# The second half of a channel MLP as seven block products for eight, and the two halves as separate stages

## The chip, the cores and the metric

The kernel runs on one core of a Trainium2 chip. The core has a matrix engine (PE, with its weight loads shown apart as PEld), a vector engine (DVE), an activation engine (ACT), a general engine (POOL) and a queue that issues transfers (SP). The metric is the device time of one execution in microseconds, the median of several. A matrix product writes to PSUM, eight banks of 2 KB for each of 128 partitions; everything else lies in SBUF or in DRAM.

## The reference, cut to what matters

One layer of a diffusion backbone is computed for 128 context tokens and 1024 sample tokens, 1152 together, at a model width of 1024. A mixer (a bidirectional scan and a gated chunk product) comes first. The change concerns what follows, the channel MLP with a squared ReLU, and the norm at the end:

```python
h = rmsnorm(x, norm2_g) * (1 + sc2) + sh2
x = x + g2 * (jnp.square(jax.nn.relu(h @ w_ff1)) @ w_ff2)   # w_ff1 (1024, 4096), w_ff2 (4096, 1024)
...
y_prompt = rmsnorm(xp, final_norm_g)                        # over the 1024 features
```

All inputs and outputs are float32. Each operand of a large product is split into a high part (rounded for the engine) and a low part (the rest), and a product is the sum of three: high by high, high by low, low by high.

## The kernel before, in words

Features lie on the 128 partitions and tokens along the rows, so an activation of 1024 features by 1152 tokens is 8 blocks of 128 rows by 1152 columns. Tokens are worked in three slices of 384 (`SL`, `NS = 3`), the hidden width of 4096 in 32 blocks of 128.

Weights come from DRAM by `wtile` (L171): a transfer of 512 KB on SP into a raw buffer, then `split` (L167), which makes the high part on ACT (a cast) and the low part on POOL (a subtraction), or on DVE where the call says so. `product` (L183) runs 24 matmuls for one output block of 128 by one slice: 8 blocks of the inner width, three matmuls each.

Ahead of the MLP, `norm2(s)` (L933) makes the MLP's input for slice `s`: one matmul with ones sums the squares over the features (`np`), ACT takes the root, DVE the reciprocal, and `modulate` (L206) then makes for each of 8 blocks a scaled value on DVE (`hn`), its high part on ACT (`h22h` for the last slice) and its low part on DVE (`h22l`).

The MLP goes over the hidden width in 16 steps of two blocks (`FB = 2`). `ff1` (L951) makes one hidden block for one slice: a `product`, ReLU on ACT, the square's high part on ACT, the square on POOL, the low part on DVE. `ff2` (L962) multiplies two hidden blocks by their rows of `w_ff2` for all 8 output blocks and 3 slices, 6 matmuls of 384 columns in one PSUM tile each, and `add_scaled` adds the tile to the residual `x1`, which stays in SBUF, by one or two DVE instructions (two where the context and the sample tokens meet in one slice). The two are interleaved: step b of `ff1` is followed by the products of step b-1 in `ff2`, so no hidden block is ever stored.

The last `ff2` call takes the last four hidden blocks and goes over the columns in three pieces (`LAST`: 448, 384 and 320 columns). While it runs, `last` and `final` make the norm of the pieces that are done: sums of squares on ACT, POOL and DVE, root, reciprocal, the scaling on DVE and POOL, and the stores.

From the end of the mixer on, a scheduler sets the order on each engine when the program is built: it takes instructions by the order of the code, lets ready ones pass, and places waits where a buffer is still in use. Each engine then works its own list strictly in that order.

## Time and profile before

| | us |
|---|---|
| median of 3 (1806.94 to 1809.33) | 1807.11 |
| the profiled execution | 1807.15 |
| its span, first to last instruction | 1805.4 |
| first matmul of `ff1` | 982.3 |
| last matmul of `ff2` starts | 1791.3 |

The page gives the busy time of each engine over the span. Matmuls are pipelined: a row's duration (334 ns for 384 columns) overlaps the next row, so what a matmul costs in a stream is the distance between starts. A table by stage gives for each stretch its length, then the busy time of PE, PEld, DVE, ACT and POOL with the count of instructions, then the granted PE clock (1.00 is 2.4 GHz, 0.50 is 1.2 GHz), the busy share of the transfer engines and what they moved; asked for one line, it counts that line's instructions alone. A timeline row has start, duration, engine, line, operation, tiles and sizes, and in brackets the idle time before it with what ended it. A row by shape has the count, the busy time and, after the comma, the mean duration in ns. A row of one tile has the shortest, the median and the longest duration in ns, and the first and last start.

### The profile page before, as it was taken

The numbers are of one execution on the slowest core, as the hardware profiler recorded it, in microseconds if no ns is written. First come the engines' busy times: TensorE is split into PE (matmuls) and PEld (weight loads), VectorE is DVE, ScalarE is ACT, GpSimd is POOL, SyncE is SP. The second block draws the span as 40 slices with busy tenths as digits, with TensorE's granted clock in tenths as the row PEclk, the third lists the DMA queues.
The fourth block names the chain that finished last, engine by engine and source line by source line (L and its number), as shares of the span: only waits on it lengthen the run. The fifth ranks groups of instructions, "written<-read, shape, count | busy, mean of one in ns | idle before, by whom it ended". The sixth has DMA issues, their size and how long they took to land.

```text
span 1805.4 us, 26426 instructions
## 1 busy us (share of the span) xinstructions
PE 1711.6 (95%) x10349; PEld 1644.1 (91%) x10349; DVE 1068.3 (59%) x1551; ACT 669.7 (37%) x1261; POOL 704.3 (39%) x493
## 2 busy tenths in 40 slices
PE   6999998898898988999999999999999999999996
PEld 3888997797888887999999999999999999999996
DVE  5956669969779789575588334344333333444427
ACT  4543446556555555453344411211222221111132
POOL 2300227637537457346555422222233332222234
PEclk9999999999999998999999999999999999999998
DMA  9676333342242364874333111111111111111103
GB/s 348 213 254 212 101 118 101 109 144 96 93 140 85 121 216 148 281 268 133 106 108 103 47 36 47 48 36 37 46 47 47 47 36 36 47 47 36 36 12 106
DMA packets 84925, 193.82 MB, mean 107 GB/s; under 512 B 7584, under 2 KB 47552, under 8 KB 84800
## 3 DMA queue, kind: packets, MB, share of 16 engines
q1 hardware_dynamic: 84800, 192.12, 32.5%
q8 instruction: 82, 1.34, 0.3%
q14 instruction: 43, 0.35, 0.1%
HBM read 157.27 MB, written 34.82 MB: 106 GB/s over the span
## 4 chain that ended last, share of the span: by engine, by line
PE 60%; DVE 14%; issue 5%; ACT 4%; POOL 1%; DMA 1%; DVEq 0%; SPq 0%; ACTq 0%; POOLq 0%
PE fps L190 22%; PE gps L969 21%; PE ops L190 7%; PE ips L190 7%; DVE ap L719 3%; DVE cv L613 2%; ACT ap L722 2%; DVE xwl L169 1%; DVE xw L696 1%; DVE M L724 1%; DVE x L987 1%; PE yp L784 1%; DVE red L929 1%; DVE h20l L216 1%; DVE x L867 0%
## 5 line engine op out<-in xcount | busy, mean ns | idle before, releaser
L867 DVE SCALAR_TENSOR_TENSOR x<-gps,modT,x 128x128 f32<-128x128 f32 (+2 forms) x480 | 232.8, 514 | 122.5 <-PE gps L969 122.5
L960 DVE TENSOR_TENSOR fl<-r,fh 128x384 fp32r<-128x384 f32 x96 | 54.1, 565 | 363.4 <-POOL r L959 363.4
L969 PE MATMUL gps<-fh,w2h 128*128 128x384 f32 (+2 forms) x768 | 257.6, 335 | 1.5 <-DVE x L867 1.5
L969 PE MATMUL gps<-fh,w2l 128*128 128x384 f32 (+2 forms) x768 | 256.9, 334 | 0.0
L969 PE MATMUL gps<-fl,w2h 128*128 128x384 f32 (+2 forms) x768 | 256.8, 334 | 0.0
L169 POOL TENSOR_TENSOR w2l<-w2r,w2h 128x1024 fp32r<-128x1024 f32 x31 | 74.5, 2403 | 324.4 <-ACT w2h L168 324.4
L168 ACT CAST w2h<-w2r 128x1024 fp32r<-128x1024 f32 x32 | 33.6, 1051 | 340.1 <-PE gps L969 314.2
L969 PEld LDWEIGHTS gps<-fh,w2h 128*128 128x128 f32 x768 | 144.2, 188 | 3.0 <-DVE x L867 2.1
L969 PEld LDWEIGHTS gps<-fl,w2h 128*128 128x128 f32 x768 | 144.2, 188 | 0.8 <-issue 0.2
L969 PEld LDWEIGHTS gps<-fh,w2l 128*128 128x128 f32 x768 | 144.1, 188 | 0.6 <-DVE w2l L169 0.2
L959 POOL TENSOR_TENSOR r<-r 128x384 f32<-128x384 f32 x96 | 79.6, 830 | 148.5 <-ACT fh L958 148.5
L169 POOL TENSOR_TENSOR wil<-wir,wih 128x1024 fp32r<-128x1024 f32 x25 | 63.7, 2549 | 161.2 <-ACT wih L168 157.3
L613 DVE SCALAR_TENSOR_TENSOR cv<-xp,cw,cv 128x1156 f32<-128x1156 f32 x64 | 109.7, 1714 | 25.3 <-ACT cv L610 24.1
L722 ACT ACTIVATE ap<-ap,lcol 128x128 f32<-128x128 f32 x288 | 89.4, 391 | 63.8 <-DVE ap L719 63.7
L957 ACT ACTIVATE r<-fps 128x384 f32<-128x384 f32 x96 | 46.8, 489 | 171.5 <-PE fps L190 170.4
L169 POOL TENSOR_TENSOR wol<-wor,woh 128x1024 fp32r<-128x1024 f32 x32 | 80.6, 2525 | 67.6 <-ACT woh L168 67.6
L169 POOL TENSOR_TENSOR w1l<-w1r,w1h 128x1024 fp32r<-128x1024 f32 x32 | 76.8, 2400 | 66.8 <-ACT w1h L168 66.8
L718 POOL TENSOR_TENSOR ea<-ea,cv 128x1024 f32<-128x1024 f32 x32 | 95.2, 2975 | 8.8 <-ACT ea L717 8.8
L190 PE MATMUL ips<-h0h,wil 128*128 128x384 f32 x256 | 90.2, 352 | 0.0
L190 PE MATMUL ips<-h0h,wih 128*128 128x384 f32 x256 | 89.9, 351 | 0.0
L190 PE MATMUL ips<-h0l,wih 128*128 128x384 f32 x256 | 89.9, 351 | 0.0
L190 PE MATMUL ips<-h1h,wil 128*128 128x384 f32 x256 | 88.2, 345 | 0.0
(292 smaller groups left out, 4915.1 us busy)
## 6 DMA issues: line engine op xcount, KB each, us to landing
wa<-in_w_ada_dram SPq DMA_DIRECT2D x48, 512.0 KB, 5.2
wor<-in_w_out_dram SPq DMA_DIRECT2D x40, 512.0 KB, 3.6
ap<-arow_d SPq DMA_DIRECT2D x36, 512.0 KB, 4.9
wir<-in_w_in_dram SPq DMA_DIRECT2D x32, 512.0 KB, 4.0
w1r<-in_w_ff_dram SPq DMA_DIRECT2D x32, 512.0 KB, 3.5
w2r<-in_w_ff_dram SPq DMA_DIRECT2D x32, 512.0 KB, 3.5
mix_d<-vg SPq DMA_DIRECT2D x9, 512.0 KB, 5.2
mxt<-mix_d SPq DMA_DIRECT2D x8, 576.0 KB, 4.5
```

The costliest lines, as they stand in the source:

```text
L168: nc.scalar.copy(hi, src)
L169: lo_eng.tensor_tensor(out=lo, in0=src, in1=hi.bitcast(F32), op=ALU.subtract)
L190: nc.tensor.matmul(ps, a[:, k, :], b[:, k, :], start=n == 0, stop=n == 3 * KD - 1)
L613: nc.vector.scalar_tensor_tensor(out=acc, in0=xp[:, k:k + 1156], scalar=cw[:, 16 * k + m:16 * k + m + 1], in1=acc, op0=ALU.mult, op1=ALU.add)
L718: nc.gpsimd.tensor_tensor(out=ea, in0=ea, in1=G.CT[:, cc(c)].unsqueeze(1).to_broadcast([P, 8, P]), op=ALU.mult)
L719: nc.vector.tensor_tensor(out=ap.rearrange("p (d e) i -> p d e i", d=2), in0=ap.rearrange("p (d e) i -> p d e i", d=2), in1=mask.unsqueeze ...
L722: nc.scalar.activation(ap[:, e, :], ap[:, e, :], AF.Exp, bias=lcol[:, c, 8 * g + e:8 * g + e + 1])
L867: nc.vector.scalar_tensor_tensor(out=x1[m][:, a:b], in0=ps[:, a - cols.start:b - cols.start], scalar=modT[:, g0 + m, v:v + 1], in1=x1[m][: ...
L957: nc.scalar.activation(r, ps, AF.Relu)
L959: nc.gpsimd.tensor_tensor(out=r, in0=r, in1=r, op=ALU.mult)
L960: nc.vector.tensor_tensor(out=fl[:, cs], in0=r, in1=fh[:, cs].bitcast(F32), op=ALU.subtract)
L969: nc.tensor.matmul(ps, a[:, m, :], x[:, cols], start=n == 0, stop=n == n1)
```

## The change

The first half of the MLP becomes a stage of its own. For each pair of hidden blocks it runs 2 by 3 products as before, writes, for each half `q` of the tokens, the ReLU of four sub-blocks (two hidden blocks by two token blocks of `TB = 288`) into a tile of seven places, squares them on ACT, forms three sums and differences on POOL, makes the high part on ACT and the low part on DVE, and stores both, 128 rows by 7 by 288 columns each (1.03 MB), in DRAM (`hid_d`). `norm2` also stores the residual in DRAM (`x1_d`).

Then the first stage's pools are closed and the second half begins. For each of 8 groups of four hidden blocks (`kb`), 4 pairs of output blocks (`m`) and 2 halves of the tokens (`q`) it runs seven block products by a form of Strassen's scheme (Winograd's), each 2 inner blocks by three matmuls of 288 columns. `hidden` loads a group's eight tiles from DRAM into a pool of 11 (`hid`); `w2_blocks` loads four blocks of `w_ff2`, forms the seven weight blocks on POOL, and splits them on ACT and DVE. The products go to two PSUM tiles of four banks each, and `evict` adds them to sums in SBUF (`acc`): four banks after the first four products, three after the other three. In the last group `assemble` makes the output blocks from the seven sums, scales them, adds the residual loaded from DRAM and sums the squares; `final` norms and stores them.

```diff
-    wp = ctx.enter_context(tc.tile_pool(name="wp", bufs=2))
-    hp = ctx.enter_context(tc.tile_pool(name="hp", bufs=6))
+    held = ExitStack()
+    wp = held.enter_context(tc.tile_pool(name="wp", bufs=2, reuse_waits="tile"))
+    hp = held.enter_context(tc.tile_pool(name="hp", bufs=6, reuse_waits="tile"))
...
+        nc.sync.dma_start(x1_d[:, :, scols(s)], x1t[:, :, scols(s)])
...
+    def ff1(f, e, R, after=None):
+        w = wtile(i["w_ff1"][f], "w1")
+        for s in range(NS):
+            ps = mps("fps")
+            product(ps, w, h2[s])
+            for t in range(2 * NQ):
+                a, b = max(t * TB, s * SL), min((t + 1) * TB, (s + 1) * SL)
+                if a < b:
+                    nc.scalar.activation(R[t // 2][:, SLOT[e][t % 2], a - t * TB:b - t * TB], ps[:, a - s * SL:b - s * SL], AF.Relu)
+            if after and s == 1:
+                after()
+    def combine(R, n, q):
+        b11, b21, b22, t1, t2, t3, t4 = (R[:, j, :] for j in range(7))
+        nc.scalar.activation(R[:, 0:4, :], R[:, 0:4, :], AF.Square)
+        for o, x, y, op in ((t3, b22, t1, ALU.subtract), (t1, t1, b11, ALU.subtract), (t2, t3, b11, ALU.add), (t4, b21, t2, ALU.subtract)):
+            nc.gpsimd.tensor_tensor(out=o, in0=x, in1=y, op=op)
+        rh = tl("rh", "rh", (7, TB), F32R)
+        lo = R.bitcast(F32R)
+        split(rh, lo, R, nc.vector)
+        nc.sync.dma_start(hid_d[n][q, 0], rh.bitcast(F32))
+        nc.sync.dma_start(hid_d[n][q, 1], R)
...
+    phase(acc=8, wr=4, wf=2, hid=11)
...
+    def w2_blocks(kb, m):
+        F = tl("wf", "wf", (2, 8, P))
+        for e in range(2):
+            for f, o in ((0, 6), (1, 0)):
+                nc.sync.dma_start(F[:, e, o:o + 2, :], i["w_ff2"][4 * kb + 2 * e + f][:, 2 * m:2 * m + 2, :])
+        a12, a22, s1, s2, s3, s4, a11, a21 = (F[:, :, j, :] for j in range(8))
+        for o, x, y, op in ((s3, a11, a21, ALU.subtract), (s1, a21, a22, ALU.add), (s2, s1, a11, ALU.subtract), (s4, a12, s2, ALU.subtract)):
+            nc.gpsimd.tensor_tensor(out=o, in0=x, in1=y, op=op)
+        wh, wl = (tl("wr", "w2" + x, (2, 7, P), F32R) for x in "hl")
+        split(wh, wl, F[:, :, 0:7, :], nc.vector)
+        return wh, wl
+    def hidden(kb, q):
+        out = []
+        for n in range(2):
+            out.append(tuple(tl("hid", "hid" + x, (7, TB), F32R) for x in "hl"))
+            for z in range(2):
+                nc.sync.dma_start(out[n][z].bitcast(F32), hid_d[2 * kb + n][q, z])
+        return out
+    def products(ps, js, w, h, first):
+        for j in js:
+            b, a, x = BANK[j], W_OF[j], H_OF[j]
             n = 0
-            for (wh, wl), (_, ah, al) in zip(ws, acts):
-                for a, x in ((wh, ah), (wh, al), (wl, ah)):
-                    nc.tensor.matmul(ps, a[:, m, :], x[:, cols], start=n == 0, stop=n == n1)
+            for e in range(2):
+                for wz, hz in ((0, 0), (0, 1), (1, 0)):
+                    nc.tensor.matmul(ps[:, b, :TB], w[wz][:, e, a, :], h[e][hz][:, x, :], start=first and n == 0, stop=n == 5,
+                                     skip_group_check=True)
                     n += 1
-            add_scaled(ps, m, cols, 40)
+    def evict(o, ps, fresh):
+        if fresh:
+            nc.scalar.copy(o, ps)
+        else:
+            nc.vector.tensor_tensor(out=o, in0=o, in1=ps, op=ALU.add)
+    def units(us, kb, done=None):
+        pss = [pf.tile([P, 4, 512], F32, tag="u", name="ups") for _ in us]
+        for (m, q, w, h), ps in zip(us, pss):
+            products(ps, (1, 7, 5, 6), w, h, True)
+            evict(acc[m][q][:, 0:4, :], ps[:, 0:4, :TB], kb == 0)
+        for (m, q, w, h), ps in zip(us, pss):
+            products(ps, (2, 4, 3), w, h, False)
+            evict(acc[m][q][:, 4:7, :], ps[:, 0:3, :TB], kb == 0)
             if done:
-                done(m, cols)
+                done(m, q)
...
+    def assemble(m, q):
+        A = acc[m][q]
+        x = tl("hid", "x", (4, TB))
+        for e in range(2):
+            nc.sync.dma_start(x[:, 2 * e:2 * e + 2, :].rearrange("p a t -> p (a t)"), x1_d[:, 2 * m + e, 2 * q * TB:2 * (q + 1) * TB])
+        nc.vector.tensor_tensor(out=A[:, 0], in0=A[:, 0], in1=A[:, 3], op=ALU.add)
+        nc.vector.tensor_tensor(out=A[:, 1], in0=A[:, 1], in1=A[:, 2], op=ALU.add)
+        nc.vector.tensor_tensor(out=A[:, 5:7], in0=A[:, 5:7], in1=A[:, 0:1].to_broadcast([P, 2, TB]), op=ALU.add)
+        nc.vector.tensor_tensor(out=A[:, 1], in0=A[:, 1], in1=A[:, 0], op=ALU.add)
+        for e, js in ((0, (4, 6)), (1, (5, 1))):
+            for t, j in enumerate(js):
+                for a, b, v in cut((2 * q + t) * TB, (2 * q + t + 1) * TB):
+                    r = slice(a - (2 * q + t) * TB, b - (2 * q + t) * TB)
+                    nc.vector.scalar_tensor_tensor(out=A[:, j, r], in0=A[:, j, r], scalar=modT[:, 40 + 2 * m + e, v:v + 1],
+                                                   in1=x[:, 2 * e + t, r], op0=ALU.mult, op1=ALU.add)
+                if sums[q] is None:
+                    sums[q] = [None, None]
+                sq = tl("hid", "sq", (TB,))
+                nc.scalar.activation(sq, A[:, j], AF.Square)
+                if sums[q][t] is None:
+                    sums[q][t] = sq
                 else:
+                    nc.gpsimd.tensor_tensor(out=sums[q][t], in0=sums[q][t], in1=sq, op=ALU.add)
+    def final(q):
+        for t in range(2):
+            ps = pf.tile([P, 4, 512], F32, tag="u", name="nps")[:, 0, :TB]
+            nc.tensor.matmul(ps, ones, sums[q][t], start=True, stop=True)
+            rs = tl("hid", "rs", (TB,))
+            nc.scalar.activation(rs, ps, AF.Sqrt, bias=eps_t, scale=1.0 / D)
+            nc.vector.reciprocal(rs, rs)
+            for e in range(2):
+                for m in range(4):
+                    o = acc[m][q][:, ((4, 6), (5, 1))[e][t]]
+                    nc.vector.scalar_tensor_tensor(out=o, in0=o, scalar=vcol("final_norm_g", 2 * m + e), in1=rs, op0=ALU.mult, op1=ALU.mult)
+                    nc.sync.dma_start(y_out[2 * m + e, :, (2 * q + t) * TB:(2 * q + t + 1) * TB], o)
...
+    for kb in range(nb - 1):
+        hs = [hidden(kb, q) for q in range(NQ)]
+        for m in range(4):
+            w = w2_blocks(kb, m)
+            units([(m, q, w, hs[q]) for q in range(NQ)], kb)
+    hs = [hidden(nb - 1, q) for q in range(NQ)]
+    for q in range(NQ):
+        for m in (0, 2):
+            units([(k, q, w2_blocks(nb - 1, k), hs[q]) for k in (m, m + 1)], nb - 1, assemble)
+        final(q)
```

Three places show what the scheduler makes of it. The first is PE where the MLP begins; `fps` is an `ff1` product, `h20`, `h21` and `h22` the input of the three slices. Before:

```order
L190 MATMUL fps<-h20h,w1l 128x384
L200 MATMUL np<-red,ones 128x384
L190 MATMUL fps<-h21h,w1h 128x384
L190 MATMUL fps<-h21l,w1h 128x384
L190 MATMUL fps<-h21h,w1l 128x384
```

Now:

```order
L195 MATMUL fps<-h21h,w1l 128x384
L205 MATMUL np<-red,ones 128x384
L195 MATMUL fps<-h22h,w1h 128x384
L195 MATMUL fps<-h20h,w1h 128x384
L195 MATMUL fps<-h20l,w1h 128x384
```

Behind `np` stood 72 matmuls that need only the first two slices; now the next matmul needs the third slice's high part, which `np` leads to.

The second is SP where one group of hidden blocks follows another in the second stage; `hid_d2` and `hid_d3` are the second group's pairs, the first `hidh` and `hidl` of a pair are the token half q = 0, the others q = 1. Before, SP issued in the MLP nothing but the weights of both halves (`w1r`, `w2r`), a step's like the next:

```order
L179 DMA w2r_10949<-in_w_ff2_dram 128x1024
L179 DMA w2r_11351<-in_w_ff2_dram 128x1024
L179 DMA w1r_11563<-in_w_ff1_dram 128x1024
L179 DMA w1r_11571<-in_w_ff1_dram 128x1024
L179 DMA w2r_11357<-in_w_ff2_dram 128x1024
L179 DMA w2r_11759<-in_w_ff2_dram 128x1024
```

Now:

```order
L1013 DMA hidh_12940<-hid_d2_107 128x2016
L1013 DMA hidl_12941<-hid_d2_107 128x2016
L999 DMA wf_12837<-in_w_ff2_dram 128x256 x4
L1013 DMA hidh_12944<-hid_d3_108 128x2016
L999 DMA wf_12956<-in_w_ff2_dram 128x256 x4
L999 DMA wf_13059<-in_w_ff2_dram 128x256 x4
L999 DMA wf_13162<-in_w_ff2_dram 128x256 x4
L1013 DMA hidl_12945<-hid_d3_108 128x2016
L1013 DMA hidh_12948<-hid_d2_107 128x2016
L1013 DMA hidl_12949<-hid_d2_107 128x2016
L1013 DMA hidh_12952<-hid_d3_108 128x2016
L1013 DMA hidl_12953<-hid_d3_108 128x2016
```

Three tiles of the group are loaded ahead; the last five take buffers of the group at work, whose tiles are read until its last pair of output blocks.

The third is DVE at the end; `acc` are the sums of one pair of output blocks, `x` the residual. Before, one instruction followed each product tile, and the last ones were:

```order
L867 SCALAR_TENSOR_TENSOR x1_7337<-gps_15873,modT_115,x1_7337 128x320
L929 TENSOR_TENSOR red_15768<-red_15768,sq_15870 128x320
L929 TENSOR_TENSOR red_15768<-red_15768,sq_15887 128x320
L867 SCALAR_TENSOR_TENSOR x1_7337<-gps_15890,modT_115,x1_7337 128x320
L203 RECIPROCAL fs_15909<-fs_15909 128x160
L203 RECIPROCAL fs_15925<-fs_15925 128x160
L987 SCALAR_TENSOR_TENSOR x1_7337<-x1_7337,vec_104,fs_15909 128x160 x5
L987 SCALAR_TENSOR_TENSOR x1_7337<-x1_7337,vec_104,fs_15925 128x160 x5
```

Now, the end of the second token half, for the last two pairs of output blocks (`acc_12509` and `acc_12511`):

```order
L1030 TENSOR_TENSOR acc_12511<-acc_12511,ups_16083 128x1152
L1052 TENSOR_TENSOR acc_12511<-acc_12511 128x288
L1053 TENSOR_TENSOR acc_12511<-acc_12511 128x288
L1055 TENSOR_TENSOR acc_12511<-acc_12511 128x288
L1030 TENSOR_TENSOR acc_12509<-acc_12509,ups_16082 128x864
L1054 TENSOR_TENSOR acc_12509<-acc_12509 128x576
L1060 SCALAR_TENSOR_TENSOR acc_12509<-acc_12509,modT_132,x_16153 128x288 x3
L1030 TENSOR_TENSOR acc_12511<-acc_12511,ups_16083 128x864
L1054 TENSOR_TENSOR acc_12511<-acc_12511 128x576
L1060 SCALAR_TENSOR_TENSOR acc_12511<-acc_12511,modT_132,x_16195 128x288 x4
L1077 RECIPROCAL rs_16220<-rs_16220 128x288
L1077 RECIPROCAL rs_16241<-rs_16241 128x288
```

The additions of `assemble` stand between the evictions of the last group, eight times in all, and sixteen scalings follow the two reciprocals for each token half.

## Rows read from the trace of the kernel before

**Rows 1.** The page, part 1: busy time, share of the span and instructions.
```profile
PE 1711.6 (95%) x10349; PEld 1644.1 (91%) x10349; DVE 1068.3 (59%) x1551; ACT 669.7 (37%) x1261; POOL 704.3 (39%) x493
```

**Rows 2.** Stretch table, line of the `ff1` products alone.
```profile
982.30:1740.70 758.40, 407.38 (x2306) 404.49 (x2304) 1.00 0.14 42
```

**Rows 3.** Stretch table, line of the `ff2` products alone, in two stretches.
```profile
1033.50:1737.00 703.50, 351.72 (x2016) 349.78 (x2017) 1.00 0.14 42
1737.00:1791.50 54.50, 51.98 (x288) 48.77 (x288) 1.00 0.16 58
```

**Rows 4.** Timeline at the end: the last matmul of `ff2`, the last DVE rows.
```profile
1791.32 0.31 PE L969 MATMUL gps<-fh,w2l 128*128 128x320 f32 x1
...
1797.04 4.05 DVE L987 SCALAR_TENSOR_TENSOR x<-x,vec,fs 128x160 f32<-128x160 f32 x10
```

**Rows 5.** PE timeline: three matmuls of 256 columns, then one of 384.
```profile
280.29 0.28 PE L704 MATMUL Sps<-xwh,Bh 128*128 128x256 f32 x1
...
280.64 0.34 PE L190 MATMUL ips<-h2h,wil 128*128 128x384 f32 x1
```

**Rows 6.** PE timeline in `ff2`: twelve matmuls of 320 columns apart.
```profile
1783.13 0.31 PE L969 MATMUL gps<-fl,w2h 128*128 128x320 f32 x1
...
1784.89 0.31 PE L969 MATMUL gps<-fl,w2h 128*128 128x320 f32 x1
```

**Rows 7.** One line's instructions: a weight load of `ff2`.
```profile
L969 PEld LDWEIGHTS gps<-fh,w2h x768: 187/188/192, 1033.5 to 1790.9; 128*128 128x128 f32 x192
```

**Rows 8.** Instructions by shape, ACT, 1033 to 1806 us.
```profile
L958 ACT ACTIVATE fh<-r 128x384 fp32r<-128x384 f32 x85 | 44.6, 525 | 2.7
L168 ACT CAST w2h<-w2r 128x1024 fp32r<-128x1024 f32 x30 | 31.5, 1051 | 335.8 <-PE gps L969 314.2 <-DMA w2r<-in_w_ff_dram 16.4 <-PE fps L190 5.2
```

**Rows 9.** Instructions by shape, POOL, 1033 to 1806 us.
```profile
L959 POOL TENSOR_TENSOR r<-r 128x384 f32<-128x384 f32 x86 | 71.3, 829 | 126.6 <-ACT fh L958 126.6
L169 POOL TENSOR_TENSOR w2l<-w2r,w2h 128x1024 fp32r<-128x1024 f32 x29 | 69.7, 2403 | 320.4 <-ACT w2h L168 320.4
```

**Rows 10.** Instructions by shape, DVE, 1033 to 1806 us.
```profile
L867 DVE SCALAR_TENSOR_TENSOR x<-gps,modT,x 128x384 f32<-128x384 f32 x232 | 141.5, 616 | 68.2 <-PE gps L969 68.2
L867 DVE SCALAR_TENSOR_TENSOR x<-gps,modT,x 128x256 f32<-128x256 f32 x112 | 53.2, 475 | 0.0
...
L203 DVE RECIPROCAL fs<-fs 128x384 f32<-128x384 f32 x1 | 2.6, 2553 | 1.2 <-ACT fs L202 1.2
L203 DVE RECIPROCAL fs<-fs 128x160 f32<-128x160 f32 x2 | 2.2, 1124 | 1.6 <-ACT fs L202 1.6
L929 DVE TENSOR_TENSOR red<-red,sq 128x320 f32<-128x320 f32 x4 | 1.9, 486 | 0.2
L169 DVE TENSOR_TENSOR w2l<-w2r,w2h 128x1024 fp32r<-128x1024 f32 x1 | 1.2, 1226 | 0.4 <-ACT w2h L168 0.4
```

**Rows 11.** Stretch table: 3 us with the transfer engines full.
```profile
39.00:42.00 3.00, 3.00 (x24) 2.34 (x22) 2.23 (x7) 2.27 (x5) 0.06 (x1) 1.00 1.01 405
```

**Rows 12.** PE timeline: the norm's matmul `np`; then tile `h22h` and `h22l`.
```profile
986.57 0.59 PE L200 MATMUL np<-red,ones 128*128 128x384 f32 x1
...
L215 ACT ACTIVATE h22h<-hn,modT x8: 617/618/619, 993.7 to 1000.5; 128x384 fp32r<-128x384 f32 x8
L216 DVE SCALAR_TENSOR_TENSOR h22l<-hn,modT,h22h x8: 605/607/619, 994.6 to 1001.2; 128x384 fp32r<-128x384 f32 x8
```

**Rows 13.** The tile `w1r` (512 KB a load): time from issue to landing.
```profile
DMA to landing us min/median/max: 3.4/3.5/4.3
```

**Rows 14.** Timeline, POOL and DVE, 979 to 980 us.
```profile
979.37 2.39 POOL L169 TENSOR_TENSOR w1l<-w1r,w1h 128x1024 fp32r<-128x1024 f32 x1 [4.72 <-ACT w1h L168]
...
979.75 2.42 DVE L929 TENSOR_TENSOR red<-red,sq 128x384 f32<-128x384 f32 x1 [0.68 <-ACT sq L928]
```

**Rows 15.** Stretch table: a pause of PE and what follows.
```profile
726.00:729.00 3.00, 1.09 (x10) 1.12 (x12) 3.00 (x3) 1.17 (x3) 2.78 (x3) 0.75 0.04 15
729.00:732.00 3.00, 3.00 (x24) 2.67 (x22) 1.15 (x3) 0.90 (x2) 1.44 (x2) 0.68 0.85 237
```

99 lines of the change are left out of this document (26 added, 73 removed).

## The prediction, made before the changed kernel ran

> **What bounds the kernel now.** I read the page's busy shares first, then the stretch tables of the two lines that do the MLP's products, then the end. PE is busy 95% of the span and DVE 59% [rows 1]. From the first `ff1` matmul at 982.3 us the `ff1` products take 407.4 us of PE and the `ff2` products 351.7 + 52.0 = 403.7 us, both at granted clock 1.00 with the transfer engines at 14 to 16% [rows 2, 3]. Span 1805.4 less 982.3 is 823.1 us, so 823.1 - 407.4 - 403.7 = 12.0 us are neither, and the end accounts for them: the last matmul starts at 1791.32 and 14.1 us of norm and stores follow [rows 4] (a few tenths of a product lie on either side). So this half of the kernel is PE from edge to edge, and nearly nothing else shows. That the products shrink must help; that anything else is put on the path must hurt. The reference is the profiled execution, 1807.15 us, which agrees with the median 1807.11.
>
> **Seven products for eight.** `ff2` has 2304 matmuls of 384 columns, 403.7 / 2304 = 0.175 us each. Now there are 8 groups x 4 x 2 x 7 x 6 = 2688 of 288 columns, and the order on PE has just that many, so the change does what it says. What 288 columns cost has no row. Starts are apart by (280.64 - 280.29) / 3 = 0.117 us at 256 columns and by 1.76 / 12 = 0.147 us at 320 [rows 5, 6], midway 0.132 us; with the rounding of the times, 0.130 to 0.136. 2688 x 0.132 = 354.8 us, 49 us less than 403.7 (384 columns would have given an eighth, 50 us). Seven groups of 336 matmuls take 310.5 us (306 to 320); the eighth goes into the last term below.
>
> A weight load has 188 ns [rows 7], longer than those distances of 117 and 147 ns, so loads overlap each other in the trace and don't set the pace at 256 and 320 columns. The Trainium skill (Perfetto Trace Analysis, § Identifying the Most-Contended Engine) takes the share of weight-load time as the measure of how near TensorE is to its limit, 91% here; by it, more and narrower matmuls would lose. That is the fifth rival.
>
> **The first half.** Its products are the same 2304 matmuls, 407.4 us. For a pair of hidden blocks PE has 407.4 / 16 = 25.5 us. Beside it, per pair: ACT some 13 us, POOL 8 x 0.65 = 5.2 us of sums beside two weight splits of 2.40, DVE two splits of 2.26 [rows 8 to 10]; all fit. The stores, 4.1 MB a pair, stand on SP ahead of weight loads of 1 MB: 5.1 MB at 405 GB/s [rows 11] is 12.7 us of 25.5. Hidden; without that cover SP would be next. Added: 0.
>
> One wait moves. `np` of the third norm runs at 986.57, the first `h22h` starts at 993.7 and lasts 0.62, the last `h22l` ends at 1001.8 [rows 12]. Before, 72 matmuls (12.6 us) that don't need them stood behind `np`; now the next matmul needs `h22h`. PE then waits 994.3 - 986.6 = 7.7 us, and follows the eight pairs as DVE makes them. I take +7 (4 to 12).
>
> **The transition.** PE has nothing from the last `ff1` product until a hidden tile has been stored and loaded back. I size by columns. ACT: 384 columns 0.525, 1024 1.051 us [rows 8], so ReLU 0.6, square of 1152 columns 1.16, cast of 2016 1.86. POOL: 384 0.829, 1024 2.403 [rows 9], so 288 are 0.65 and four 2.6. DVE: two inputs from SBUF, 320 columns 0.486, 1024 1.226 [rows 10], so 2016 are 2.26. Chain 0.6 + 1.16 + 2.6 + 1.86 + 2.26 = 8.5 us. Then on SP come the stores of the last pair, the first weights and eight loads of 1.03 MB. A load of 512 KB lands 3.5 us after its issue [rows 13]; at 405 GB/s it needs 1.3 of them, so 2.2 us are fixed and a tile in a stream costs 2.5 us. A product over the first inner pair needs two tiles, over both pairs four, the second half eight. With the stores ahead of them the fourth lands about 24 us after the last `ff1` matmul, the eighth about 34; the 46 matmuls possible between take 6.1. So +28 (22 to 38): 22 if the first groups' tiles, long in DRAM, start early enough, 38 if store and load don't overlap.
>
> **Between groups.** Eight tiles are in use and `hid` has 11 places, so five of the next eight loads wait for the last products of q = 0 in the old group. They land 4.7, 7.2, 9.7, 12.3 and 14.8 us later (2.2 fixed, 2.5 each) [rows 11, 13]; PE meanwhile has 18 matmuls of the old group (2.4 us) and those of the new group that need three tiles. Walking the new order against the landings leaves waits of 1.8, 1.5, 1.3 and 0.4 us, 5 us for a boundary. Six of them (the seventh is in the last term): +30 (12 if the three tiles ahead carry it, 54 if PE waits until the fifth). Inside a group, per pair of output blocks PE has 84 x 0.132 = 11.1 us; DVE has evictions and a split. Evictions from PSUM: 256 columns 0.475, 384 0.616 [rows 10], so 1152 are 1.41 and 864 1.12; 2 x 2.53 + 2.03 = 7.1 us. Hidden, at 64%.
>
> One row bears on that margin. A DVE sum of 384 columns took 2.42 us where POOL was in a 2.39 us subtraction that had begun 0.38 us earlier [rows 14]; its like took about half a microsecond without (320 columns 0.486 [rows 10]). The Trainium skill (SBUF — State Buffer, § Who interferes with whom) says that a DVE instruction with two SBUF inputs and a POOL instruction that reads SBUF share a port, and that whichever starts first holds it to its end; the trace agrees. By that rule the evictions, with one input in PSUM, are free of POOL. Mid-group POOL works 2.4 of 11.1 us; in the last group it has 8 x 2.4 + 28 x 0.65, about 37 us, beside DVE's additions, scalings and splits.
>
> **The last group and the end.** Here DVE carries more than PE, from the order's counts and the prices above: 8 evictions of each size 20.2; 7 splits 14.2; 24 additions of 288 columns (0.46) 11; 8 of 576 (0.76) 6.1; scalings with the residual 18.3 (288 columns by the 384-column 0.62 and 320-column row: 0.52, five pieces for a pair of blocks at q = 0, four at q = 1); 4 reciprocals of 288, between 1.12 at 160 and 2.55 at 384 [rows 10], 1.94 each, 7.8; 32 last scalings 16.5. Sum 94 us, against PE's 336 x 0.132 = 44.4. DVE works its list in order: an eviction stands behind the additions of the pair before, PE behind that eviction, and in the middle the reciprocals of the first token half wait for POOL's sums and a matmul with all of the second half's evictions behind them. Waits on top: 5 for the first eviction, 4 for the residual's loads (its tiles take `hid` places), 2 x 3.3 for the norms' chains, 2 for the last store, and 8 for meetings with POOL, a fifth of its 37 us. 94 + 25.6 = 119.6, so 120 us from the end of group 7 (95 with hardly a wait; 145 if each POOL instruction holds DVE). Before, the same stretch was an end of 14 us.
>
> **The sum.** 407.4 + 7 + 28 + 310.5 + 30 + 120 = 902.9 against 823.1: +79.8. Ahead of 982.3 nothing of weight moves (-2 to +5). 1807.15 + 79.8 = 1887 us. Matmuls give back 49; four places take 129.
>
> **Rivals.**
> 1. *The clock falls in the new pauses.* In 726 to 729 PE was busy 1.09 of 3 us and the clock 0.75; the next 3 us were full at 0.68 [rows 15]. Such a pause costs 1.7 to 3.4 us of half speed. One transition, seven boundaries and the last group's waits give 20 to 28: 1907 to 1915. Against: 5 us in pieces is a shorter pause than that one.
> 2. *Milder.* The loads find gaps and the last group's DVE work spreads: transition 22, boundaries 15, last 100, norm 4: 860 + 8 of other waits, 1845 to 1852.
> 3. *Faster.* The other side, by one mechanism: PE's queue remains the only bound to the end because DVE's list in the last group keeps pace with it. Then 407.4 + 8 + 20 + 354.8 + an end of 24 = 814, 9 less: 1798. It decides at DVE work of about 56 us there, not 94 (a price per column 40% under the rows), with boundaries that cost nothing. No row is that cheap.
> 4. *Same.* A mixture of 2 and 3 that comes out within 0.2%: only by accident.
> 5. *Weight loads set the pace.* 188 ns for each of 2688 [rows 7] instead of 132: 150 us more, 2037. Against it: the distances of 117 and 147 ns [rows 5, 6].
>
> **How the numbers follow.** Forecast 0.70 (1842 to 1935: the ends of the terms taken together as independent give 1855 to 1924, widened for the last group, whose order has no row like it), clock 0.14, milder 0.07, faster 0.05, same 0.02, weight loads 0.02. The range 1842 to 1935 takes in the first three. 0.2% is about what a measurement of this kernel can tell from no change: faster 0.05, same 0.02, slower 0.70 + 0.14 + 0.07 + 0.02 = 0.93.
>
> **What would show it.** Starts of 288-column matmuls 0.132 us apart inside a group (0.188 would be rival 5); PE idle at each group's start, ended by loads of the hidden tiles; DVE near full in the last 110 us, PE under half; a gap of some 28 us between the stages; clock 1.00 except there. I am wrong if DVE waits for PE in the last group, or if the boundaries are closed, and too low if the granted clock stays under 1 behind them.

## The result, and the profile after

The changed kernel takes 1905.76 us (1904.19 to 1908.21), the kernel before beside it 1807.03 us: ratio 1.0545, 95% interval 1.0527 to 1.0564. The forecast was 1887 (1842 to 1935): the sign and most of the mechanisms held, the sum was 19 us short. The profiled execution has a span of 1903.3 us, against 1805.4. One execution of one later run (4209.62 us, PE slow from its start, cause open) is left out of every number below.

The page's busy line, to be held against [rows 1]:

```profile
PE 1696.0 (89%) x10729; PEld 1615.0 (85%) x10729; DVE 1097.9 (58%) x1234; ACT 753.0 (40%) x1344; POOL 787.6 (41%) x638
```

PE has less busy time than before and a longer span: the matmuls did shrink, and PE now waits. The stretch table by stage (length, then busy time and instructions of PE, PEld, DVE, ACT, POOL, then granted clock, transfer share, GB/s) says where: the first half, the pause after it, the first group, one middle group, the last group with the end.

```profile
984.30:1396.00 411.70, 407.08 (x2307) 405.73 (x2306) 80.13 (x49) 169.04 (x291) 187.65 (x153) 1.00 0.50 192
1396.00:1419.40 23.40, 0.14 (x1) 0.00 (x0) 5.36 (x3) 7.04 (x6) 7.28 (x10) 0.60 0.77 285
1419.40:1480.90 61.50, 52.00 (x336) 50.00 (x337) 9.93 (x5) 21.50 (x19) 20.72 (x24) 0.85 0.56 212
1480.90:1531.50 50.60, 46.00 (x338) 44.67 (x337) 26.03 (x19) 7.56 (x5) 10.92 (x15) 1.00 0.54 204
1785.70:1903.30 117.60, 60.38 (x346) 54.76 (x344) 96.73 (x132) 27.48 (x43) 48.34 (x48) 0.75 0.41 143
```

Inside a group matmuls start 0.132 us apart, as forecast; sixteen of them on PE's timeline, first and last:

```profile
1499.83 0.29 PE L1022 MATMUL ups<-hidh,w2l 128*128 128x288 f32 x1
...
1501.95 0.29 PE L1022 MATMUL ups<-hidh,w2h 128*128 128x288 f32 x1
```

(1501.95 - 1499.83) / 16 = 0.1325 us. A group's 336 matmuls are 44.4 us; the six middle groups take 304.8 us together. So against the terms of the forecast:

| | forecast, us | measured, us |
|---|---|---|
| before 982.3 | 0 | +2.0 |
| first half with the norm's pause | 414.4 | 411.7 |
| transition: pause, and the first group above 44.4 | 28 | 23.5 + 17.1 = 40.6 |
| seven groups of matmuls | 310.5 | 7 x 44.4 = 310.8 |
| six boundaries | 30 | 304.8 - 6 x 44.4 = 38.4 |
| last group and end | 120 | 117.6 |

Two terms were too small, the transition by 12.6 and the boundaries by 8.4. The first `ff1` matmul starts between 982.6 and 986.8 us in the later runs, none of which touches what lies ahead of it, so the +2.0 is scatter.

### The profile page after: what moved, and what is told of

The parts are those of the page before. It is cut to its first block, busy times and chain, and to the rows that moved or that the text cites. A ratio compares the mean times of both kernels' runs of the same rounds, so it can differ in the third digit from the quotient of the medians.

```text
span 1903.3 us, 27353 instructions
## 1 busy us (share of the span) xinstructions
PE 1696.0 (89%) x10729; PEld 1615.0 (85%) x10729; DVE 1097.9 (58%) x1234; ACT 753.0 (40%) x1344; POOL 787.6 (41%) x638
## 5 line engine op out<-in xcount | busy, mean ns | idle before, releaser
L1022 PE MATMUL ups<-hidh,w2h 128*128 128x288 f32 x896 | 274.8, 308 | 62.6 <-DVE acc L1030 26.7
L1022 PE MATMUL ups<-hidl,w2h 128*128 128x288 f32 x896 | 270.4, 302 | 13.1 <-DMA hidl<-hid_d 13.1
L1022 PE MATMUL ups<-hidh,w2l 128*128 128x288 f32 x896 | 269.0, 301 | 4.5 <-DVE w2l L174 4.5
L1002 POOL TENSOR_TENSOR wf<-wf 128x256 f32<-128x256 f32 x144 | 113.4, 797 | 306.1 <-DMA wf<-in_w_ff_dram 288.7
L1022 PEld LDWEIGHTS ups<-hidh,w2h 128*128 128x128 f32 x896 | 173.7, 194 | 72.4 <-ACT w2h L173 33.3
L1030 DVE TENSOR_TENSOR acc<-acc,ups 128x1152 f32<-128x1152 f32 (+1 forms) x112 | 133.5, 1201 | 133.7 <-PE ups L1022 133.6
L1022 PEld LDWEIGHTS ups<-hidl,w2h 128*128 128x128 f32 x896 | 174.3, 195 | 15.5 <-DMA hidl<-hid_d 15.3
L1022 PEld LDWEIGHTS ups<-hidh,w2l 128*128 128x128 f32 x896 | 174.0, 194 | 5.6 <-DVE w2l L174 5.6
L972 POOL TENSOR_TENSOR r<-r 128x288 f32<-128x288 f32 x128 | 102.5, 811 | 104.9 <-ACT r L970 99.9
L618 DVE SCALAR_TENSOR_TENSOR cv<-xp,cw,cv 128x1156 f32<-128x1156 f32 x64 | 109.6, 1713 | 25.4 <-ACT cv L615 24.1
L174 DVE TENSOR_TENSOR w2l<-wf,w2h 128x1792 fp32r<-128x1792 f32 x36 | 76.3, 2121 | 77.1 <-ACT w2h L173 61.5
L963 ACT ACTIVATE r<-fps 128x288 f32<-128x288 f32 (+2 forms) x192 | 52.8, 329 | 102.4 <-PE fps L195 102.4
L195 PE MATMUL fps<-h22h,w1h 128*128 128x384 f32 x256 | 86.7, 339 | 4.6 <-ACT h22h L220 4.6
## 6 DMA issues: line engine op xcount, KB each, us to landing
hidl<-hid_d SPq DMA_DIRECT2D x32, 1008.0 KB, 10.7
```

Of the source, the lines that this page charges most:

```text
L174: lo_eng.tensor_tensor(out=lo, in0=src, in1=hi.bitcast(F32), op=ALU.subtract)
L195: nc.tensor.matmul(ps, a[:, k, :], b[:, k, :], start=n == 0, stop=n == 3 * KD - 1)
L618: nc.vector.scalar_tensor_tensor(out=acc, in0=xp[:, k:k + 1156], scalar=cw[:, 16 * k + m:16 * k + m + 1], in1=acc, op0=ALU.mult, op1=ALU.add)
L963: nc.scalar.activation(R[t // 2][:, SLOT[e][t % 2], a - t * TB:b - t * TB], ps[:, a - s * SL:b - s * SL], AF.Relu)
L972: nc.gpsimd.tensor_tensor(out=o, in0=x, in1=y, op=op)
L1002: nc.gpsimd.tensor_tensor(out=o, in0=x, in1=y, op=op)
```

## Experiments

### What the seven products are worth

One product of each unit is worked twice.

```diff
             products(ps, (1, 7, 5, 6), w, h, True)
+            products(ps, (6,), w, h, False)
```

> One of the seven block products is worked twice, so that each unit has eight, 3072 matmuls and not 2688; the output is not the layer's. Theory (matmuls at 0.132 us are what the first seven groups are made of): 48 x 0.132 = 6.3 us more in each of them, 44 us, and at most 3 in the last group, where DVE and waits hide PE: 1948 to 1953 us. Rival (the groups' length is set by loads or DVE that would hide the added matmuls): less than 30 us more, below 1936 us.

Measured: 1951.47 us, 45.7 more. The six middle groups take 345.3 us, 40.5 or 6.75 each more, the last 2.3 more. 48 more matmuls at 0.132 us are 6.3 us a group, so PE's matmuls are what the middle groups are made of, and the scheme's saving is real: nearly 46 us against eight products in this same structure. The loss lies around them.

### The boundaries

First, all groups use the first group's hidden tiles.

```diff
+    hs = [hidden(0, q) for q in range(NQ)]
     for kb in range(nb - 1):
-        hs = [hidden(kb, q) for q in range(NQ)]
...
-    hs = [hidden(nb - 1, q) for q in range(NQ)]
```

> The eight hidden tiles of the first group are loaded once and used by all eight groups; the other 56 loads are left out, so the output is not the layer's. In the changed kernel a middle group takes 50.6 to 51.0 us, of which the 336 matmuls are 44.4, three waits at its start 4.5 and two later ones 1.0. Theory (the loads of the next group's tiles come late, since five of eight wait for places): the three waits go, a group takes 45.5 to 46.5 us, six of them give back 26 to 32 us and the kernel takes 1872 to 1880 us. Rival (the waits at a group's start are those for the first pair's weight blocks or for evictions, and only coincide with the loads): a group stays at 49.5 us or above, the kernel above 1896 us. Second rival (the transfers also slow what lies beside them): the two later waits go too, 44.5 us a group, below 1870 us.

Second, a real cure: two pairs of output blocks for one token half, then for the other, so that half of the tiles come free 84 matmuls before a group's end.

```diff
-    phase(acc=8, wr=4, wf=2, hid=11)
+    phase(acc=8, wr=6, wf=2, hid=10)
...
-        for m in range(4):
-            w = w2_blocks(kb, m)
-            units([(m, q, w, hs[q]) for q in range(NQ)], kb)
+        for m in (0, 2):
+            w = [w2_blocks(kb, m + e) for e in range(2)]
+            for q in range(NQ):
+                units([(m + e, q, w[e], hs[q]) for e in range(2)], kb)
```

> Whole computation. In the first seven groups the units go over two pairs of output blocks for one token half, then for the other, so that the tiles of q = 0 come free 84 matmuls (11.1 us) before the group's end and not 18 (2.4 us); hid has 10 places, the weight blocks 6. Theory of late loads: four tiles land 12.2 us after the first issue, so a wait of about 1 us is left, a middle group takes 45.5 to 47.5 us and six give back 20 to 30 us; the first group gains a few us as well, since the tiles of q = 1 are wanted later: 1872 to 1884 us. Rival (the weight blocks then bind: two sets are in use for 22 us, and the fourth set of a group waits for a place, then 3.7 us of ACT and DVE): two waits of up to 4 us in a group, as much as is saved, 1900 to 1912 us.

Measured: 1866.51 and 1861.44 us. A middle group of the first, and one of the second:

```profile
1482.90:1527.30 44.40, 44.40 (x338) 44.40 (x337) 25.95 (x19) 7.56 (x5) 11.78 (x16) 1.00 0.16 48
```
```profile
1476.50:1521.10 44.60, 44.58 (x337) 44.58 (x338) 25.70 (x20) 7.43 (x5) 11.62 (x16) 1.00 0.61 233
```

All of the 6.4 us per boundary are gone in both, with the transfers taken away and with them kept (share 0.61). So it was not the transfers' bandwidth. The theory had expected some 1 us of waits to stay in either run, and that went as well: the second rival of the first run was right in its number, and the second run shows why it is not a matter of traffic.

What PE waited for in the six middle groups of the changed kernel is in its list of waits (total, times, longest), and it is mostly not a load:

```profile
PE ups L1022 <- DVE acc L1030: 18.7, 23, 1.3
PE ups L1022 <- DMA hidl<-hid_d: 8.8, 6, 1.6
PE ups L1022 <- DMA hidh<-hid_d: 1.0, 1, 1.0
```

The start of one group shows how the two belong together. SP issues the group's late tiles from 1478.21 on, 2.7 us before the old group's end at 1480.9; then come PE's first three waits, and DVE's evictions behind them:

```profile
1478.21 0.33 SPq L1013 DMA_DIRECT2D hidl<-hid_d  x1
...
1480.59 0.32 SPq L1013 DMA_DIRECT2D hidl<-hid_d  x1
```
```profile
1482.97 0.40 PE L1022 MATMUL ups<-hidl,w2h 128*128 128x288 f32 x1 [1.36 <-DMA hidl<-hid_d]
...
1487.32 0.40 PE L1022 MATMUL ups<-hidh,w2h 128*128 128x288 f32 x1 [1.32 <-DVE acc L1030]
...
1491.37 0.40 PE L1022 MATMUL ups<-hidh,w2h 128*128 128x288 f32 x1 [1.15 <-DVE acc L1030]
```
```profile
1485.91 1.35 DVE L1030 TENSOR_TENSOR acc<-acc,ups 128x1152 f32<-128x1152 f32 x1 [1.13 <-PE ups L1022]
1490.26 1.05 DVE L1030 TENSOR_TENSOR acc<-acc,ups 128x864 f32<-128x864 f32 x1 [3.00 <-PE ups L1022]
```

The first wait ends with a tile. The other two end with evictions that DVE, idle until then, began as soon as PE let it: an eviction of four banks, then one of three, so PE has a single unit (seven products for one pair of output blocks and one token half) in hand and nothing to do while its sums are read out. In both runs above the evictions of a group come two and two, and PE's list of waits for the middle groups is empty. One of the first run's groups, with a split directly before the evictions:

```profile
1484.71 2.02 DVE L174 TENSOR_TENSOR w2l<-wf,w2h 128x1792 fp32r<-128x1792 f32 x1 [9.08 <-ACT w2h L173]
1486.66 1.35 DVE L1030 TENSOR_TENSOR acc<-acc,ups 128x1152 f32<-128x1152 f32 x1
1489.45 1.35 DVE L1030 TENSOR_TENSOR acc<-acc,ups 128x1152 f32<-128x1152 f32 x1 [1.44 <-PE ups L1022]
```

So late tiles cost a boundary in two ways: PE waits for one of them, and the order made for them leaves evictions uncovered. The two later waits of a group also end with evictions. The second run changed both the time at which places come free and which units stand side by side; the two were not tried apart. The first run loses the waits without the second's two more weight places.

### The transition

The last pair of hidden blocks is neither combined nor stored (the last group reads the fifteenth pair in its place).

```diff
-            combine(R[q], n, q)
+            if n < DFF // P // 2 - 1:
+                combine(R[q], n, q)
...
-                nc.sync.dma_start(out[n][z].bitcast(F32), hid_d[2 * kb + n][q, z])
+                nc.sync.dma_start(out[n][z].bitcast(F32), hid_d[min(2 * kb + n, DFF // P // 2 - 2)][q, z])
```

> The sums, splits and stores of the last of the sixteen pairs of hidden blocks are left out (the last group reads the fifteenth pair in its place), so the output is not the layer's. In the changed kernel 23.5 us lie between the last product of the first half and the first of the second, and the first group is 17.1 us longer than its matmuls. Theory (the loads of the second half stand on SP behind the last pair's stores, whose chain is both token halves one after the other, 12.5 us, and not the 8.5 of one half): the pause shrinks by 10 to 14 us to 10 to 14, the first group changes by less than 4: 1888 to 1896 us. Rival (the weight blocks or the eight tiles' transfers set it, 9 us and 22 us by themselves): less than 5 us comes back, 1900 us or more.

Measured: 1897.27 us, 8.5 less; neither number. The pause grew to 29.0 us, the first group shrank from 61.5 to 48.5: 33.1 for 40.6 together. SP's and POOL's timelines of the changed kernel, and then of this run, tell why:

```profile
1400.60 3.70 POOL L972 TENSOR_TENSOR r<-r 128x288 f32<-128x288 f32 x4 [3.63 <-ACT r L970]
1408.52 0.32 SPq L977 DMA_DIRECT2D hid_d<-r  x1
1408.89 3.20 SPq L999 DMA_DIRECT2D wf<-in_w_ff_dram  x4
1412.14 0.49 SPq L1013 DMA_DIRECT2D hidh<-hid_d  x1
...
1416.58 0.44 SPq L1013 DMA_DIRECT2D hidl<-hid_d  x1
```
```profile
1396.46 0.42 SPq L1014 DMA_DIRECT2D hidh<-hid_d  x1
...
1402.16 12.56 SPq L1000 DMA_DIRECT2D wf<-in_w_ff_dram  x6
1419.85 5.17 POOL L1003 TENSOR_TENSOR wf<-wf 128x256 f32<-128x256 f32 x7 [38.77 <-DMA wf<-in_w_ff_dram]
```

In the changed kernel the last store goes out 12.5 us after the last product, both token halves one behind the other; then 3.2 us of weight issues; then eight tiles, 8 x 1.03 MB, by an estimate at 405 GB/s [rows 11] 20 us. The stretch table has the transfers full and the clock halved in that pause of the changed kernel:

```profile
1408.00:1414.00 6.00, 0.00 (x0) 0.00 (x0) 0.49 (x1) 0.00 (x0) 0.20 (x1) 0.50 1.00 353
```

Without the chain the tiles went out 15.3 us sooner after the last product, but ahead of half of the first weight block, whose sums could begin only at 1419.85. Stores, weights and tiles are issued on one queue, and with one taken away the next bound.

Next, the loads themselves are moved. The token half q = 0 of the first group and the first weight block get places over the residual's, which is free in SBUF all through the first half, and the last pair's sums go to DVE. (This run starts from the kernel with pairs and small places, 1858.73 us, shown under the last group.)

```diff
-    phase(r=4, rh=2, m=4)
+    phase(m=4, r=4, rh=2)
...
-    phase(acc=8, wr=6, wf=2, hid=9, s=7)
+    phase(acc=8, wr=4, s=7, wf=1, hq=4, hid=5, wg=1, wq=2)
...
+        if kb == 0:
+            with tc.high_priority():
+                first = w2_blocks(0, 0)
+                hs = [hidden(0, 0)]
+            hs.append(hidden(0, 1))
...
-            nc.gpsimd.tensor_tensor(out=o, in0=x, in1=y, op=op)
+            (nc.vector if n == DFF // P // 2 - 1 else nc.gpsimd).tensor_tensor(out=o, in0=x, in1=y, op=op)
```

> Whole computation. As with pairs and small places (1858.7 us; 27.7 us from the last product of the first half to the first of the second, and 9.9 more in the first group), but the places of the first group's q = 0 tiles and of the first weight block lie over the residual's, which is free from the first half's start, so that they are loaded before the last pair's stores; and the last pair's sums are made on DVE. Theory (the pause is a chain and eight loads one after the other on SP; with four of the eight loaded, PE can start after the weight split, some 5 us, and then waits for q = 1's tiles at about 25 us): 15 to 22 us less, 1837 to 1844 us. Rival (the tiles of q = 1 end at the same time as before, so that the pause only moves behind the first 84 matmuls): 11 us less at most, 1848 us or more.

Measured: 1850.50 us, 8.2 less: the rival. PE starts 3.5 us after the last product and not 27.5, but the first group grows from 54.3 to 65.7. On PE's timeline (idle time before a row in brackets) the pause has moved to where the second weight block and the other half's tiles are wanted:

```profile
1400.41 0.40 PE L1030 MATMUL ups<-hidh,w2h 128*128 128x288 f32 x1 [3.32 <-ACT r L963]
...
1417.60 0.61 PE L1030 MATMUL ups<-hidh,w2h 128*128 128x288 f32 x1 [5.50 <-ACT w2h L173]
1419.79 0.58 PE L1030 MATMUL ups<-hidh,w2h 128*128 128x288 f32 x1 [1.33 <-DMA hidh<-hid_d]
```

Half of what was hoped. SP's timeline has the first tile of q = 1 out at 1412.17, behind the last store (1408.54) and four more weight issues, almost when it was out before (1412.14). That these tiles wait for the places of the first half's last tiles is how the places were laid out; it was not tried apart from their place on the queue.

### The last group

Four runs on the claim that DVE's list bounds it. In the first the first token half's norm is called later.

```diff
+            if q == 1 and m == 0:
+                final(0)
-        final(q)
+    final(1)
```

> Whole computation. The norm of the first token half is called after the first two pairs of the second half and not before them, so its two matmuls no longer stand ahead of the second half's products on PE. The changed kernel has one pause of 19 us on PE there, 16.5 of it for POOL's sums of squares. Theory (DVE's list bounds the last group: 96.7 us busy of 117.6): PE's pause is mostly cover, and what can be saved is DVE's own idle time around it, 4.3 and 3.4 us: 0 to 8 us less, 1898 to 1906 us. Rival (PE's queue, blocked by the norm's matmul, is what sets the end): 14 to 19 us less, 1887 to 1892 us.

Measured: 1903.49 us, 2.3 less, about as much as the executions scatter (1900.68 to 1906.65). The largest pause of PE in the whole stage,

```profile
1840.71 2.76 PE L1074 MATMUL nps<-sq,ones 128*128 128x288 f32 x4 [16.54 <-POOL sq L1069]
```

was worth hardly anything. PE's waits for the squares fell from 24.1 to 10.7 us in this stage, and its waits for DVE's evictions grew from 8.0 to 15.6: the wait is long, but others stood behind it. The second leaves out the additions of `assemble`.

```diff
-        nc.vector.tensor_tensor(out=A[:, 0], in0=A[:, 0], in1=A[:, 3], op=ALU.add)
-        nc.vector.tensor_tensor(out=A[:, 1], in0=A[:, 1], in1=A[:, 2], op=ALU.add)
...
```

> The 32 additions of assemble (24 of 288 columns, 8 of 576) are left out, so the output is not the layer's. They are 20.9 us of DVE's time in the last group. Theory (DVE's list bounds the last group): 17 to 24 us less, 1882 to 1889 us, and DVE still busy 75% or more of what is left. Rival (the norm's chain through POOL and the residual's loads set the end, DVE only waits with them): at most 8 us less, 1898 us or more.

Measured: 1899.28 us, 6.5 less, where DVE alone would have given 17 or more. The stage now is

```profile
1782.10:1892.00 109.90, 57.71 (x346) 52.75 (x344) 76.87 (x100) 27.45 (x43) 43.52 (x48) 0.79 0.44 153
```

so DVE's idle time grew from 21 to 33 us. That was a miss: DVE has the most work, but its list is not the bound. The third gives the squares small places (and works from the pairs).

```diff
-    phase(acc=8, wr=6, wf=2, hid=10)
+    phase(acc=8, wr=6, wf=2, hid=9, s=7)
...
-                sq = tl("hid", "sq", (TB,))
+                sq = tl("s", "sq", (TB,))
...
-            rs = tl("hid", "rs", (TB,))
+            rs = tl("s", "rs", (TB,))
```

> Whole computation. As the kernel with pairs of output blocks and token halves (1861 us, last group and end 115.4 us), but the squares, their sums and the norm's factors, which took places of 8 KB in hid, get a pool of seven small tiles; hid has 9 places, so that the residual's tiles no longer wait for a square to be summed on POOL. Leaving out 21 us of DVE's additions gave only 7.8 us in the last group, so DVE's list alone is not its bound. Theory (places in hid: residual's loads wait for POOL and for DVE, and the weight loads behind them on SP): the last group and end take 98 to 108 us, the kernel 1844 to 1855 us. Rival (DVE and POOL hold each other up on the squares and weight sums, whatever the places): 112 us or more, 1857 us or more.

Measured: 1858.73 us, 2.7 less than with pairs; the stage 111.0 us, between the two numbers, the kernel on the rival's side. The waits for the residual's loads (7.0 us of DVE's in the run with pairs) are gone, and others came. The fourth takes the additions from this one.

```diff
-        nc.vector.tensor_tensor(out=A[:, 0], in0=A[:, 0], in1=A[:, 3], op=ALU.add)
-        nc.vector.tensor_tensor(out=A[:, 1], in0=A[:, 1], in1=A[:, 2], op=ALU.add)
...
```

> The 32 additions of assemble are left out again, this time where the squares have small places of their own (1858.7 us, last group and end 111 us, DVE busy 95.8); the output is not the layer's. Theory (two bounds in turn, DVE's list and the residual's places; with the places settled only DVE is left): 15 to 22 us less, 1837 to 1844 us, twice what the same edit gave with the old places (6.5 us). Rival (PE, the weight blocks or the norm's chain bind as well): 4 to 9 us less again, 1850 us or more.

Measured: 1851.64 us, 7.1 less: the rival again, so places were not the second bound. The chain that ended last, in the kernel with small places, suggests what was (start, length, what):

```profile
1760.96 0.73 POOL wf L1002
1761.69 0.98 POOL sq L1069
1762.67 0.93 POOL wf L1002
...
1765.32 1.61 ACT w2h L173
```

POOL's sums of the next weight block are interleaved with its sums of squares, and PE and DVE wait behind. In the last group every weight block is made twice, once for each token half: 8 x 4 sums on POOL and 8 splits on DVE. The last run, on top of the early loads, makes them once, calls the first half's norm just before the last unit's results are assembled, and brings the third slice's norm forward for the first pair only.

```diff
-        for e in range(2):
-            ff1(2 * n + e, e, R, (lambda: norm2(NS - 1)) if n == e == 0 else None)
+        for e, s in ((0, 0), (0, 1), (1, 0), (1, 1), (0, 2), (1, 2)) if n == 0 else [(e, s) for e in range(2) for s in range(NS)]:
...
+            if n == e == s == 0:
+                norm2(NS - 1)
...
-    for q in range(NQ):
-        for m in (0, 2):
-            units([(k, q, w2_blocks(nb - 1, k), hs[q]) for k in (m, m + 1)], nb - 1, assemble)
-        final(q)
+    for m in (0, 2):
+        w = [w2_blocks(nb - 1, m + e) for e in range(2)]
+        for q in range(NQ):
+            def done(k, q):
+                assemble(k, q)
+                if (k, q) == (2, 1):
+                    final(0)
+            units([(m + e, q, w[e], hs[q]) for e in range(2)], nb - 1, done)
+    final(1)
```

> Whole computation. As with the early loads (1850.5 us), and with two more edits. The third slice's norm is early for the first pair of hidden blocks alone; the two tries that interleaved both blocks in all sixteen pairs lost 47 to 53 us, since both weight places were in use until a pair's end and PE waited 2.5 us in 14 pairs for POOL's split of the next. And the last group goes over pairs like the others, so that its weight blocks are made four times and not eight, with the first half's norm behind the products. Theory (the last group is bound by DVE's list and by POOL's weight sums behind the squares, of which this takes 8 us each; the norm's pause was 5.6 us): the first half within 1 us of 408, the last group and end 97 to 103 us and not 112, the kernel 1832 to 1841 us; it stays slower than the kernel before. Rival (the last group is bound by the chain of the norm and PE's half clock): 108 us or more there, 1844 us or more.

Measured: 1830.80 us, 19.7 less than before these edits, 75.0 less than the changed kernel; against the kernel before 1.0121 (1.0104 to 1.0138), so still 1.2% slower. The last stage of the kernel that it builds on, with early loads, and of this one:

```profile
1733.20:1845.10 111.90, 59.94 (x346) 55.71 (x344) 92.80 (x132) 24.99 (x42) 46.94 (x48) 0.74 0.40 136
```
```profile
1735.00:1829.90 94.90, 51.11 (x346) 47.74 (x344) 84.34 (x128) 19.12 (x38) 27.47 (x32) 0.79 0.40 139
```

17.0 us less, somewhat more than the theory's 9 to 15, with 8.5 of DVE's time and 19.5 of POOL's taken out; DVE is now busy 89% and POOL 29%. That fits a stage bound by DVE and POOL in turn: 20.9 us from DVE alone gave some 7, 8.5 from DVE together with POOL's share gave 17. It is not shown by itself, since how the 17 us divide between the weight blocks and the place of the norm was not tried apart; the norm alone had given 2.3 in the older order. What the half clock costs this stage (granted clock 0.75 there in the changed kernel, 0.79 in this one) was not tried either.

### The norm ahead of the MLP

The third slice's norm is asked for earlier, and the products of the two hidden blocks of a pair are interleaved as in the kernel before.

```diff
...
-        for e in range(2):
-            ff1(2 * n + e, e, R, (lambda: norm2(NS - 1)) if n == e == 0 else None)
+        w1 = [wtile(i["w_ff1"][2 * n + e], "w1") for e in range(2)]
+        for e, s in ((0, 0), (0, 1), (1, 0), (1, 1), (0, 2), (1, 2)):
+            ff1(s, w1[e], e, R)
+            if n == e == s == 0:
+                norm2(NS - 1)
```

> Whole computation. The third slice's norm is asked for after the first product of the first pair, and the products over the first two slices of both blocks come before those of the third, as in the kernel before. Theory (the wait behind the norm's matmul, one pause of 5.6 us and eight short ones, is the whole difference of the first half): 3.5 to 6 us less, 1900 to 1902 us. Rival (the first half is also slower for its stores or its ACT and POOL work): the pause goes but the first half stays above 409 us; within 2 us of the changed kernel.

Measured: 1952.3 us, the median of four executions between 1947.80 and 1954.58, 46.6 more. The profile kept shows none of the four and said nothing of the cause, so the edit was run again on the kernel with small places.

> Whole computation. The early norm of the third slice, this time in the kernel with pairs of output blocks and small places (1858.7 us). The first try of this edit, in the changed kernel, gave 1948 to 1955 us and once 4210, with weight loads at 0.32 us and matmuls 0.43 us apart at granted clock 1.00 through the whole execution, the mixer's too, which the edit doesn't touch. Theory (that was a disturbed chip, and the pause of 5.6 us behind the norm's matmul is the whole difference of the first half): 3.5 to 6 us less, 1852 to 1856 us, first half within 1 us of 407.5. Rival (the edit itself slows the program): 1890 us or more, in the first half.

Measured: 1911.54 us, 52.8 more: the rival, so the edit itself is slow. The first half, 466.9 us long, and the waits of PE in it from 1026 us on (total, times, longest):

```profile
986.75:1453.70 466.95, 426.13 (x2307) 416.24 (x2306) 81.42 (x50) 174.32 (x292) 185.42 (x162) 0.97 0.44 172
```
```profile
PE fps L195 <- POOL w1l L174: 35.0, 14, 2.5
```

The waits are 35 of the 55 us by which this half is longer than in the kernel with small places (412.0); another 16 us are what 121 matmuls lost that started more than 0.2 us apart, with the granted clock at 0.58 in the 3 us behind one such wait (1080 to 1083 us). The interleaving that the norm was moved by keeps both weight places in use until a pair's end, so the next pair's split on POOL starts late, in each of 14 pairs. In the last run above, with the interleaving in the first pair only, the norm's wait is gone (`h22h` starts at 992.9, the third slice is wanted at 1001.3), and one such wait of 2.5 + 2.5 us for the weights took its place: the first half is 413.3 us for 411.7. Nothing was won.

## Why the prediction was right, and where it was short

**Seven for eight** held in every number: matmuls 0.132 us apart at full clock, 44.4 us a group, the first half beside its stores still PE's alone (407.08 us busy of 411.70). The weight-load rival fell: the group without transfers above has PEld busy 44.40 of 44.40 us, all of the time, and still starts a matmul every 0.132 us. The Trainium skill (Perfetto Trace Analysis, § Identifying the Most-Contended Engine) reads that share, beside the useful work done, as nearness to the limit. Here it stood at its top and the distance between starts still went with the columns: 0.117, 0.132, 0.147 and 0.175 us at 256, 288, 320 and 384.

**Transition**, 28 for 40.6, beyond the 38 of its bound. The step that was too small is the chain: 8.5 us was worked out for one token half, and the two halves go through POOL and ACT one after the other, 12.5 us. Four sums of 288 columns on POOL took 3.3 and 3.7 us, not 2.6: the forecast's 0.65 a sum lies a little above the straight line through the two rows of 384 and 1024 columns [rows 9], which gives 0.59, and the sums took 0.81. And SP's four small weight issues took 3.2 us, a cost that no term had. To this comes the clock rival in small: the granted clock was 0.50 in the pause, and 41 matmuls of the first group started 0.2 to 0.3 us apart, 4.4 us above 41 x 0.132. These are pieces read from one trace; taking the chain away gave back 7.5 us of the 40.6.

**Boundaries**, 30 for 38.4, nearer than the reasoning deserves. The walk of the order against the landings gave 5 us in four waits, all for tiles. In the group above PE waits once for a tile (1.5 us beyond the matmuls' own distance) and then twice for evictions (2.8 together), which the forecast had put at nothing ("Hidden, at 64%"); that the three come to 4.3, close to its 5, is luck. The other 1.9 us are two later waits, also for evictions (1.1), and after each wait a second matmul that starts 0.24 us behind the first (0.8 in all). The clock stayed at 1.00, so here that rival fell.

**The last group**, 120 for 117.6, is right in size and wrong in part of its reason. The counts and prices were good (94 us of DVE forecast, 96.7 measured), but the stage was called DVE's alone with waits on top. Taking 20.9 us of DVE's work out gave only 6.5 and 7.1. The chain that ended last has DVE in 56 of the stage's 118 us, POOL's sums of squares and weight sums in 17, loads of weights, residual and tiles in another 17; POOL was busy 48.3 us there, 37 were forecast. DVE's idle time came to 20.9 us for a forecast 25.6 of waits, near it, though only in part for the reasons given. The meetings of DVE and POOL were priced from [rows 14] and are seen here, the same addition alone and beside POOL:

```profile
1792.65 0.45 DVE L1053 TENSOR_TENSOR acc<-acc 128x288 f32<-128x288 f32 x1
...
1805.64 1.00 DVE L1053 TENSOR_TENSOR acc<-acc 128x288 f32<-128x288 f32 x1
```

POOL was in two sums from 1805.27 for 1.96 us when the second began.

**The norm** was 4.3 us (411.7 - 407.4), at the lower end of 4 to 12.

The milder rival (1845 to 1852) did not come about in the kernel as built; with places, order and queue arranged for it, the same scheme takes 1831 us, below even that. Of the 71 us that it then still pays (transition 26, last group above its matmuls 50 where the end before was 12, norm 6), the scheme gives back 49. No version tried beats the kernel before.

## What to carry to other kernels

Fewer products pay only what their surroundings leave: price a split into stages by its seams (last chain, store, load, first weights on one queue) before counting matmuls. At a seam ask when the places come free and what PE has in hand until then, not only how fast the transfers are: an order that frees half of the tiles early and keeps two units side by side removed 38 us at no cost in traffic. And the longest wait in a stage need not be the one on the path: a pause of 16.5 us of PE was worth about 2. Where a chain passes through several engines, as it seems to here, work taken off one of them shows only in part.

## What was not expected of the hardware

POOL's operations hardly got shorter from 384 columns to 288: 0.83 us for a square at 384 [rows 9], 0.81 for a sum at 288. At 256, in two pieces of 128, the mean of all was 0.80, and the median in the middle groups 0.74 (shapes, count, then busy time and mean ns; then one line's shortest, median and longest duration in ns):

```profile
L1002 POOL TENSOR_TENSOR wf<-wf 128x256 f32<-128x256 f32 x144 | 113.4, 797 | 306.1 <-DMA wf<-in_w_ff_dram 288.7
...
L972 POOL TENSOR_TENSOR r<-r 128x288 f32<-128x288 f32 x128 | 102.5, 811 | 104.9 <-ACT r L970 99.9
```
```profile
L1002 POOL TENSOR_TENSOR wf<-wf x97: 732/739/2402, 1479.7 to 1784.9; 128x256 f32<-128x256 f32 x97
```

PE's weight loads were busy 100% of a stretch in which 288-column matmuls were not slowed by them. In a pause of 23.5 us the granted clock fell to 0.50, which cost 4.4 us afterwards, and some of the waits of 2.5 us in the first half of one run also brought it down, while waits of 1.0 to 1.6 us in the middle groups left it at 1.00.
